# A decoder trunk in float32 on one Trainium2 core: seven products of sums in place of eight in the MLP's down-projection

## The chip, the core and the metric

The kernel runs on one core of one Trainium2 chip. The engines are TensorE (PE; PEld is its loading of weights), VectorE (DVE), ScalarE (ACT), GpSimd (POOL) and SyncE (SP, which issues nearly all DMAs here). The metric is the device time of one execution in microseconds (us), lower is better. A profile of one execution on the same chip gives the times of single instructions.

## The reference

Two layers. Each has a mixer (layer 0 an attention with forget gates, layer 1 a short gated convolution), a squared-ReLU MLP, and gated embeddings, with norms before and after each part. Sequence 512, width 1024, MLP width 4096, all in float32. The change concerns the MLP:

```python
def sq_relu_mlp(h, w_up, w_down):
    return jnp.square(jax.nn.relu(h @ w_up)) @ w_down

for i in range(2):
    ...                                   # mixer: x = x + rmsnorm(m, g[1])
    f = sq_relu_mlp(rmsnorm(x, g[2]), w_mlp_up[i], w_mlp_down[i])
    x = x + rmsnorm(f, g[3])
    ...                                   # gated embeddings
```

## The kernel before

**Products.** Each float32 operand is split into a high part `hi` (rounded to the matmul's fp32r form, a copy on ScalarE, L170) and a low part `lo` (source minus high part, a subtraction on VectorE, L171). `mm3` makes one product of three matmuls, `hi hi`, `lo hi` and `hi lo` (L162 to L164), all into one PSUM bank. There are eight banks of 128 x 512.

**The weight stream.** `plan` lists all weight tiles of 128 x 512 in the order of their use. `fetch` has SP load them into a ring of eight buffers (`raws`), `prepare` splits them into two pages (`wh`, `wl`), and `wide` and `narrow` hand a tile to a matmul, after they have prepared the next SOON = 8 tiles of the list. All other tiles of 128 x 512 come from a pool of PAGES = 76 pages. A tile scheduler sets the order of the instructions on each engine from the program and its own estimate of times; each engine then runs its list in order and waits on semaphores.

**The MLP.** `mlp` works through eight groups of 512 hidden columns. In a group, `up(gr)` makes four banks (index f, 128 hidden columns by all 512 tokens) of 8 x 3 matmuls each. From each bank come `r` = relu (ScalarE, L642), `hh` = its square rounded (ScalarE, L643), `q` = its square in full (VectorE, L645) and `hl` = q - hh (VectorE, L648). `down(gr, hs, t, n)` makes the bank of 128 tokens (t, four of them) by 512 output columns (n, two of them): four products over f, so 8 x 4 x 3 = 96 matmuls a group. A bank is added to the accumulator `acc[t, n]` on VectorE (L666; in group 0 copied there by ScalarE, L663). In group 0 the up stage runs in two halves of 256 tokens, since the norm before it ends block by block.

**Round about it.** `pre_norm` makes the normed input (`stats`, `rstd` with two small GpSimd instructions, L185 and L188, then `scaled` and a transposition that `put_off` defers and `need` calls in). `mixer_out` adds the mixer's output to the residual `xs` (eight pages, kept through the MLP like the gains g3 and g4). After group 7's bank pair of a token block come `squares`, `gained` and `residual`, and the next norm. `late` loads and splits the embeddings at group 7.

Of the kernel before, what the change touches and what calls it, by code (L numbers as in the profile page):

```python
# [49 lines left out]
def trunk(ctx: ExitStack, tc, x, pT, g, wv, wqk, bf, wo, wci, cw, wco, wup, wdn, wpp, wpg, out):  # L50
# [117 lines left out]
    def split(hi, lo, src):  # L168

        nc.scalar.copy(hi, src)  # L170
        nc.vector.tensor_tensor(out=lo, in0=src, in1=hi.bitcast(F32), op=ALU.subtract)  # L171
# [400 lines left out]
    def conv(hT):  # L572
# [49 lines left out]
        return lambda k, t: ys[k].at(lambda h: h[:, t * P : (t + 1) * P])  # L622

    def mlp(l, hT, xs, gB, then, late):
        acc = {}

        def up(gr):
            hs = {}
            for lo, hi in ((0, 256), (256, 512)) if gr == 0 else ((0, 512),):
                n = hi - lo  # L630
                for f in range(4):
                    need(*range(lo // P, hi // P))
                    ps = bank(f"up{l}_{gr}_{f}_{lo}")
# [8 lines left out]
                    nc.scalar.activation(r[:, :n], ps[:, :n], AF.Relu)  # L642
# [2 lines left out]
                    nc.vector.tensor_tensor(  # L645
                        out=sq[:, :n], in0=r[:, :n], in1=r[:, :n], op=ALU.mult
                    )
                    nc.vector.tensor_tensor(  # L648
# [188 lines left out]
```

## Time and profile before

| what | value |
|---|---|
| median of 3 executions | 1287.08 us (1285.12 to 1288.13) |
| the profiled execution's own time | 1285.32 us |
| its span, first to last instruction | 1283.6 us |
| mean granted clock of TensorE in it | 0.998 |
| PE busy | 1257.1 us in 6140 matmuls |
| VectorE, ScalarE, GpSimd busy | 709.7, 546.7, 151.2 us |
| moved by DMA | 140.24 MB |

In rows of the profile's groups, "out<-in" are names of the program with numbers left out, then sizes, the count after an x, and behind the bar the busy time in us, the mean of one in ns, and the idle time of the engine just before them with what ended it. A row of a timeline has its start in us, its duration in us, and then the same. A row of windows has, for each engine, the busy time and the number of instructions, then the granted clock and the share of the DMA engines.

### The profile page before, as it was taken

To read this page: it belongs to the slowest core of one execution; us is meant where nothing else is said; L and a number is where in the kernel's file an instruction comes from. 1 tells how busy PE (TensorE), PEld (TensorE's weight loads), DVE (VectorE), ACT (ScalarE), POOL (GpSimd) and SP (SyncE) were. 2 spreads that over 40 slices of the span, in tenths; PEclk is the share of its full clock that TensorE was granted. 3 is DMA by queue.
4 is the path that set the end of the run, shared out by engine and by line. 5 is a ranking of instruction groups with operands and counts; after the bars stand their busy time and mean duration, and the time that the engine had idled before them with its cause. 6 is when DMAs were issued, how large, how long until landed. Compare 5 with 4: busy or idle time off the path is not lost.

```text
span 1283.6 us, 17353 instructions
## 1 busy us (share of the span) xinstructions
PE 1257.1 (98%) x6140; PEld 1058.0 (82%) x6140; DVE 709.7 (55%) x1310; ACT 546.7 (43%) x1165; POOL 151.2 (12%) x267
## 2 busy tenths in 40 slices
PE   7999999999999999999999999999999999999997
PEld 6888888788888888888788988889888888888876
DVE  5557887573534553465867444455345444534773
ACT  5457776564422242234555233335423322432551
POOL 2026666120000000000211000010000000000120
PEclk9999999999999999999999999999999999999999
DMA  6455544533413431342323233423334123413401
GB/s 209 156 148 160 165 146 116 181 96 95 146 34 99 131 117 48 99 148 98 99 86 99 79 95 97 153 83 100 98 99 132 52 97 115 131 35 114 148 17 49
DMA packets 81174, 140.24 MB, mean 109 GB/s; under 512 B 9600, under 2 KB 16816, under 8 KB 81088
## 3 DMA queue, kind: packets, MB, share of 16 engines
q1 hardware_dynamic: 80880, 138.88, 34.8%
q8 instruction: 48, 0.79, 0.3%
q14 instruction: 38, 0.31, 0.1%
q10 hardware_dynamic: 144, 0.26, 0.1%
q0 software_dynamic: 64, 0.00, 0.0%
HBM read 132.73 MB, written 2.18 MB: 105 GB/s over the span
## 4 chain that ended last, share of the span: by engine, by line
PE 92%; DVE 3%; DMA 2%; ACT 1%; issue 1%; POOL 1%; SPq 0%; DVEq 0%; POOLq 0%; ACTq 0%
PE dn L163 9%; PE dn L162 9%; PE dn L164 9%; PE up L164 9%; PE up L162 9%; PE up L163 9%; PE qk L163 2%; PE qk L162 2%; PE qk L164 2%; PE pg L163 2%; PE pg L164 2%; PE pg L162 2%; PE pT L432 1%; PE c L164 1%; PE c L162 1%; PE u L164 1%
## 5 line engine op out<-in xcount | busy, mean ns | idle before, releaser
L171 DVE TENSOR_TENSOR wl<-raw,wh 128x512 fp32r<-128x512 f32 (+1 forms) x428 | 271.2, 686 | 49.6 <-ACT wh L170 48.8
L170 ACT CAST wh<-raw 128x512 fp32r<-128x512 f32 (+1 forms) x428 | 236.6, 614 | 23.7 <-DMA raw<-in_wdn 13.4
L163 PE MATMUL dn<-wh,hl 128*128 128x512 f32 x512 | 199.3, 389 | 0.0
L164 PE MATMUL dn<-wl,hh 128*128 128x512 f32 x512 | 199.3, 389 | 0.0
L642 ACT ACTIVATE r<-up 128x512 f32<-128x512 f32 (+1 forms) x72 | 39.7, 551 | 364.2 <-PE up L164 341.3
L162 PE MATMUL dn<-wh,hh 128*128 128x512 f32 x512 | 194.8, 389 | 0.0
L645 DVE TENSOR_TENSOR q<-r 128x512 f32<-128x512 f32 (+1 forms) x72 | 45.6, 633 | 210.0 <-ACT r L642 209.9
L666 DVE TENSOR_TENSOR acc<-dn,acc 128x512 f32<-128x512 f32 x112 | 76.9, 690 | 88.2 <-PE dn L164 88.2
L162 PEld LDWEIGHTS dn<-wh,hh 128*128 128x128 f32 x512 | 96.1, 188 | 20.0
L164 PEld LDWEIGHTS dn<-wl,hh 128*128 128x128 f32 x512 | 96.1, 188 | 19.9
L163 PEld LDWEIGHTS dn<-wh,hl 128*128 128x128 f32 x512 | 96.1, 188 | 19.8
L162 PE MATMUL up<-m0h,wh 128*128 128x512 f32 (+1 forms) x288 | 105.2, 366 | 1.4 <-ACT m0h L170 1.4
L162 PE MATMUL up<-m1h,wh 128*128 128x512 f32 (+1 forms) x288 | 105.1, 366 | 0.9 <-ACT m1h L170 0.9
L164 PE MATMUL up<-m0l,wh 128*128 128x512 f32 (+1 forms) x288 | 104.7, 366 | 0.9 <-DVE m0l L171 0.9
L163 PE MATMUL up<-m1h,wl 128*128 128x512 f32 (+1 forms) x288 | 105.0, 366 | 0.0
L163 PE MATMUL up<-m0h,wl 128*128 128x512 f32 (+1 forms) x288 | 105.0, 366 | 0.0
L164 PE MATMUL up<-m1l,wh 128*128 128x512 f32 (+1 forms) x288 | 104.5, 366 | 0.0
L185 POOL TENSOR_SCALAR mr_r_v<-fs,fs 128x1 f32<-128x1 f32 x8 | 3.9, 488 | 671.2 <-ACT junk L193 671.0
L162 PEld LDWEIGHTS up<-m0h,wh 128*128 128x128 f32 x288 | 54.3, 189 | 10.7 <-ACT m0h L170 1.9
L162 PEld LDWEIGHTS up<-m1h,wh 128*128 128x128 f32 x288 | 54.3, 189 | 9.9 <-ACT m1h L170 1.1
L164 PEld LDWEIGHTS up<-m0l,wh 128*128 128x128 f32 x288 | 54.1, 189 | 10.0 <-DVE m0l L171 1.3
L163 PEld LDWEIGHTS up<-m0h,wl 128*128 128x128 f32 x288 | 54.3, 189 | 8.7
(211 smaller groups left out, 2442.5 us busy)
## 6 DMA issues: line engine op xcount, KB each, us to landing
raw<-in_wup SPq DMA_DIRECT2D x128, 256.0 KB, 3.2
raw<-in_wdn SPq DMA_DIRECT2D x128, 256.0 KB, 4.0
raw<-in_wci SPq DMA_DIRECT2D x48, 256.0 KB, 3.2
raw<-in_wqk SPq DMA_DIRECT2D x32, 256.0 KB, 3.6
raw<-in_wpg SPq DMA_DIRECT2D x32, 256.0 KB, 3.4
g<-in_g SPq DMA_DIRECT2D x22, 256.0 KB, 5.2
prl<-neg_c SPq DMA_DIRECT2D x16, 256.0 KB, 6.0
raw<-in_wo SPq DMA_DIRECT2D x16, 256.0 KB, 3.2
```

Of the source, the lines that this page charges most:

```text
L162: nc.tensor.matmul(ps, a.hi, b.hi, start=start, stop=False)
L163: nc.tensor.matmul(ps, a.lo, b.hi, start=False, stop=False)
L164: nc.tensor.matmul(ps, a.hi, b.lo, start=False, stop=stop)
L170: nc.scalar.copy(hi, src)
L171: nc.vector.tensor_tensor(out=lo, in0=src, in1=hi.bitcast(F32), op=ALU.subtract)
L185: nc.gpsimd.tensor_scalar(out=v, in0=parts[0], scalar1=parts[1], scalar2=EPS, op0=ALU.add, op1=ALU.add)
L432: nc.tensor.transpose(ps[:, b * P : (b + 1) * P], probs[h][b][:, j * P : (j + 1) * P], ident)
L642: nc.scalar.activation(r[:, :n], ps[:, :n], AF.Relu)
L645: nc.vector.tensor_tensor(out=sq[:, :n], in0=r[:, :n], in1=r[:, :n], op=ALU.mult)
L666: nc.vector.tensor_tensor(out=a, in0=ps, in1=a, op=ALU.add)
```

## The change

In groups 0 to 6 of each layer the down-projection is a product of a 2 x 2 block matrix by another, made with seven products (Strassen's scheme in Winograd's form). A is the squared relu: A11 and A21 are the first and second half of the 512 tokens for an even f, A12 and A22 for the following odd f; the pair of f is counted by p (two in a group). B is the weight: rows r by the parity of f, columns by n. The sums are

```
S1 = A21 + A22   S2 = S1 - A11   S3 = A11 - A21   S4 = A12 - S2
T1 = B12 - B11   T3 = B22 - B12  T2 = B22 - T1    T4 = B21 - T2
products: 1: A11 B11   2: A12 B21   3: S4 B22   4: A22 T4   5: S1 T1   6: S2 T2   7: S3 T3
```

(T4 has the sign with which the combination needs additions only.) Each product has two banks (s, 128 tokens of the half each) and sums over p: 7 x 2 x 2 x 3 = 84 matmuls a group. The seven products are accumulated over groups 0 to 6 in 14 pages, and combined once per layer. Group 7 keeps the plain form, adds its banks to the combined totals, and has its first token block in another loop order. All sums T and S, the low parts of the T's and the combination run on GpSimd. The A side's high parts are copies on ScalarE of `q` and of the sums, with the low parts on VectorE. `raws` grows from 8 to 14 buffers, the pages go from 76 to 70. `xs` is written to DRAM after the mixer and read back before group 7, and g3 and g4 are loaded there.

```diff
-PAGES = 76
+PAGES = 70
+RAWS = 14
...
+PRODUCTS = {
+    1: ("A11", "B11"), 2: ("A12", "B21"), 3: ("S4", "B22"), 4: ("A22", "T4"),
+    5: ("S1", "T1"), 6: ("S2", "T2"), 7: ("S3", "T3"),
+}
+STEPS = (1, 2, 4, 5, 6, 7, 3)
...
+    def plan_down(l, gr):
+        at = {}
+        for name, r, c in (("B11", 0, 0), ("B21", 1, 0), ("B12", 0, 1), ("B22", 1, 1)):
+            for p in range(2):
+                at[name, p] = len(loads)
+                loads.append(wdn[l, c, 4 * gr + 2 * p + r])
+        for i in STEPS:
+            name = PRODUCTS[i][1]
+            for p in range(2):
+                where["dn", l, gr, name, p] = len(order)
+                order.append((("dn", l, gr, name, p), at if name[0] == "T" else at[name, p]))
+        derived[l, gr] = at
...
+    def derive(l, gr):
+        at = derived.pop((l, gr))
+        fetch(max(at.values()) + 1)
+        B = {key: fetched[n][:, :S] for key, n in at.items()}
+        for p in range(2):
+            for name, a, b in (("T1", "B12", "B11"), ("T3", "B22", "B12"), ("T2", "B22", "T1"),
+                               ("T4", "B21", "T2")):
+                t = page(f"{name}_{l}_{gr}_{p}")
+                derived[l, gr, name, p] = t
+                B[name, p] = t[:, :S]
+                nc.gpsimd.tensor_tensor(out=B[name, p], in0=B[a, p], in1=B[b, p], op=ALU.subtract)
...
-    def split(hi, lo, src):
+    def split(hi, lo, src, eng=nc.vector):
         nc.scalar.copy(hi, src)
-        nc.vector.tensor_tensor(out=lo, in0=src, in1=hi.bitcast(F32), op=ALU.subtract)
+        eng.tensor_tensor(out=lo, in0=src, in1=hi.bitcast(F32), op=ALU.subtract)
...
+        def quarters(gr, f, q, s, A):
+            L, R = slice(0, S // 2), slice(S // 2, S)
+            sums = lambda out, a, b, op: nc.gpsimd.tensor_tensor(out=out, in0=a, in1=b, op=op)
+            if f % 2 == 0:
+                halves(gr, f, ("A11",), q[f], A)
+                s[f] = page(f"s34{l}_{gr}_{f}")
+                sums(s[f][:, L], q[f][:, L], q[f][:, R], ALU.subtract)
+                return
+            left, right = q[f - 1], q[f]
+            halves(gr, f, ("A12", "A22"), right, A)
+            s12, s34 = page(f"s12{l}_{gr}_{f}"), s[f - 1]
+            sums(s12[:, L], left[:, R], right[:, R], ALU.add)
+            sums(s12[:, R], s12[:, L], left[:, L], ALU.subtract)
+            sums(s34[:, R], right[:, L], s12[:, R], ALU.subtract)
+            halves(gr, f, ("S1", "S2"), s12, A)
+            halves(gr, f, ("S3", "S4"), s34, A)
+
+        def down(gr, A):
+            for i in STEPS:
+                a_name, b_name = PRODUCTS[i]
+                banks = [bank(f"dn{l}_{gr}_{i}{s}") for s in range(2)]
+                for p in range(2):
+                    w = wide("dn", l, gr, b_name, p)
+                    for s in range(2):
+                        mm3(
+                            banks[s], A[a_name, p].at(lambda h: h[:, s * P : (s + 1) * P]), w,
+                            p == 0, p == 1,
+                        )
+                for s in range(2):
+                    if gr == 0:
+                        acc[i, s] = page(f"acc{l}_{i}_{s}")
+                        nc.scalar.copy(acc[i, s][:, :S], banks[s])
+                    else:
+                        a = acc[i, s][:, :S]
+                        nc.vector.tensor_tensor(out=a, in0=banks[s], in1=a, op=ALU.add)
+
+        def combine():
+            for s in range(2):
+                for to, i in ((2, 1), (6, 1), (7, 6), (4, 7), (6, 5), (3, 6), (5, 7)):
+                    a = acc[to, s][:, :S]
+                    nc.gpsimd.tensor_tensor(out=a, in0=a, in1=acc[i, s][:, :S], op=ALU.add)
...
+        gB = late()
+        total = combine()
...
+        for t in range(NB):
+            for n in range(2):
+                nc.sync.dma_start(kept[l, t, n], xs[t][n][:, :S])
+
+        def late():
+            for t in range(NB):
+                for n in range(2):
+                    xs[t][n] = page(f"xd{l}_{t}_{n}")
+                    nc.sync.dma_start(xs[t][n][:, :S], kept[l, t, n])
+            g3 = gain(l, 3)
+            g4.extend(gain(l, 4))
+            ps_in.extend(embeddings(l))
+            return g3
```

How it moves instructions shows in the engines' lists. Names carry the layer, the group and f or p, then a running number. GpSimd in layer 0, before: between the last statistics of the norm ahead of the MLP (`n20_r3`) and the first of the norm behind it (`mr0_r0`) its list has nothing.

```order
L185 TENSOR_SCALAR n20_r3_v_3674<-n20_q0_3_3670,n20_q1_3_3672 128x1
L188 TENSOR_TENSOR n20_r3_y_3675<-n20_r3_v_3674,neg_half_81 128x1
L185 TENSOR_SCALAR mr0_r0_v_6554<-fs0_0_0_6548,fs0_0_1_6550 128x1
L188 TENSOR_TENSOR mr0_r0_y_6555<-mr0_r0_v_6554,neg_half_81 128x1
L185 TENSOR_SCALAR n40_r0_v_6564<-n40_q0_0_6560,n40_q1_0_6562 128x1
L188 TENSOR_TENSOR n40_r0_y_6565<-n40_r0_v_6564,neg_half_81 128x1
```

GpSimd after, group 4 of layer 0, from the low parts of T4 and T1 on to those of T2 and T3:

```order
L217 TENSOR_TENSOR wl168_5611<-T4_0_4_0_5506,wh168_5610 128x512
L217 TENSOR_TENSOR wl169_5621<-T4_0_4_1_5514,wh169_5620 128x512
L217 TENSOR_TENSOR wl170_5631<-T1_0_4_0_5500,wh170_5630 128x512
L217 TENSOR_TENSOR wl171_5641<-T1_0_4_1_5508,wh171_5640 128x512
L705 TENSOR_TENSOR s340_4_2_5657<-q0_4_2_5481 128x256
L705 TENSOR_TENSOR s120_4_3_5691<-q0_4_2_5481,q0_4_3_5482 128x256
L705 TENSOR_TENSOR s120_4_3_5691<-s120_4_3_5691,q0_4_2_5481 128x256
L705 TENSOR_TENSOR s340_4_2_5657<-q0_4_3_5482,s120_4_3_5691 128x256
L217 TENSOR_TENSOR wl172_5706<-T2_0_4_0_5504,wh172_5705 128x512
L217 TENSOR_TENSOR wl173_5716<-T2_0_4_1_5512,wh173_5715 128x512
L217 TENSOR_TENSOR wl174_5730<-T3_0_4_0_5502,wh174_5729 128x512
L217 TENSOR_TENSOR wl175_5740<-T3_0_4_1_5510,wh175_5739 128x512
```

Where the list had gone straight from one norm to the next, it now has 24 instructions a group; here the sums of the second pair of f stand between the low parts of T4 and T1 and those of T2 and T3.

VectorE at the end of group 4's up stage and the beginning of its down stage, before:

```order
L645 TENSOR_TENSOR q0_4_2_0_5356<-r0_4_2_0_5353 128x512
L648 TENSOR_TENSOR hl0_4_2_5352<-q0_4_2_0_5356,hh0_4_2_5351 128x512
L645 TENSOR_TENSOR q0_4_3_0_5389<-r0_4_3_0_5386 128x512
L648 TENSOR_TENSOR hl0_4_3_5385<-q0_4_3_0_5389,hh0_4_3_5384 128x512
L171 TENSOR_TENSOR wl148_5396<-raw148_5393,wh148_5395 128x512
L171 TENSOR_TENSOR wl149_5405<-raw149_5402,wh149_5404 128x512
L171 TENSOR_TENSOR wl150_5414<-raw150_5411,wh150_5413 128x512
L171 TENSOR_TENSOR wl151_5423<-raw151_5420,wh151_5422 128x512
L171 TENSOR_TENSOR wl152_5476<-raw152_5473,wh152_5475 128x512
L171 TENSOR_TENSOR wl153_5485<-raw153_5482,wh153_5484 128x512
L171 TENSOR_TENSOR wl154_5494<-raw154_5491,wh154_5493 128x512
L666 TENSOR_TENSOR acc0_0_0_4061<-dn0_4_0_0_5392,acc0_0_0_4061 128x512
```

VectorE at the same place after:

```order
L677 TENSOR_TENSOR q0_4_2_5481<-r0_4_2_0_5650 128x512
L217 TENSOR_TENSOR A11l0_4_2_5654<-q0_4_2_5481,A11h0_4_2_5653 128x256
L677 TENSOR_TENSOR q0_4_3_5482<-r0_4_3_0_5684 128x512
L217 TENSOR_TENSOR A12l0_4_3_5688<-q0_4_3_5482,A12h0_4_3_5687 128x512
L217 TENSOR_TENSOR S1l0_4_3_5696<-s120_4_3_5691,S1h0_4_3_5695 128x512
L738 TENSOR_TENSOR acc0_1_0_4079<-dn0_4_10_5703,acc0_1_0_4079 128x512
L217 TENSOR_TENSOR S3l0_4_3_5700<-s340_4_2_5657,S3h0_4_3_5699 128x512
L738 TENSOR_TENSOR acc0_1_1_4081<-dn0_4_11_5704,acc0_1_1_4081 128x512
L738 TENSOR_TENSOR acc0_2_0_4105<-dn0_4_20_5727,acc0_2_0_4105 128x512
L738 TENSOR_TENSOR acc0_2_1_4107<-dn0_4_21_5728,acc0_2_1_4107 128x512
L738 TENSOR_TENSOR acc0_4_0_4131<-dn0_4_40_5751,acc0_4_0_4131 128x512
L217 TENSOR_TENSOR wl176_5754<-raw146_5496,wh176_5753 128x512
```

The low parts of the sums (`S1l`, `S3l`) stand between the squares and the accumulations, and the list waits there for GpSimd's sums `s12` and `s34`; the weights' low parts come behind the accumulations of products 1 and 2 (the first of them in the last row).

PE in group 4's down stage, before, where the last hidden block (`hh0_4_3`) is first used, 25 matmuls after the stage's first:

```order
L162 MATMUL dn0_4_2_0_5444<-wh141_5227,hh0_4_1_5294 128x512
L163 MATMUL dn0_4_2_0_5444<-wh141_5227,hl0_4_1_5295 128x512
L164 MATMUL dn0_4_2_0_5444<-wl141_5228,hh0_4_1_5294 128x512
L162 MATMUL dn0_4_2_0_5444<-wh142_5239,hh0_4_2_5351 128x512
L162 MATMUL dn0_4_0_0_5392<-wh143_5251,hh0_4_3_5384 128x512
L162 MATMUL dn0_4_1_0_5430<-wh143_5251,hh0_4_3_5384 128x512
L163 MATMUL dn0_4_2_0_5444<-wh142_5239,hl0_4_2_5352 128x512
```

PE at the corresponding place after, where the last hidden block (`A12h0_4_3`) is first used, 30 matmuls after the stage's first:

```order
L208 MATMUL dn0_4_11_5704<-wh165_5526,A11h0_4_2_5653 128x512
L210 MATMUL dn0_4_50_5775<-wl170_5631,S1h0_4_1_5601 128x512
L209 MATMUL dn0_4_10_5703<-wh165_5526,A11l0_4_2_5654 128x512
L210 MATMUL dn0_4_10_5703<-wl165_5527,A11h0_4_2_5653 128x512
L209 MATMUL dn0_4_11_5704<-wh165_5526,A11l0_4_2_5654 128x512
L210 MATMUL dn0_4_11_5704<-wl165_5527,A11h0_4_2_5653 128x512
L208 MATMUL dn0_4_51_5776<-wh170_5630,S1h0_4_1_5601 128x512
L209 MATMUL dn0_4_51_5776<-wh170_5630,S1l0_4_1_5602 128x512
L210 MATMUL dn0_4_51_5776<-wl170_5631,S1h0_4_1_5601 128x512
L208 MATMUL dn0_4_20_5727<-wh167_5546,A12h0_4_3_5687 128x512
L208 MATMUL dn0_4_21_5728<-wh167_5546,A12h0_4_3_5687 128x512
```

PE goes through the first pair of f for products 1, 2, 4 and 5 with eight banks open, and returns to them with the second pair; product 5's sum `S1` of the first pair and the low part `wl170` of T1 come before the last hidden block.

More of the change, by code (lines that the diff above doesn't have):

```diff
@@ L652, in up @@
-            return hs
-        def down(gr, hs, t, n):
-            ps = bank(f"dn{l}_{gr}_{t}_{n}")
-            for f in range(4):
-                mm3(
-                    ps, hs[f].at(lambda h: h[:, t * P : (t + 1) * P]),
-                    wide("dn", l, gr, n, f, soon=16 if gr == 7 else SOON), f == 0, f == 3,
-                )
-            if gr == 0:
-                acc[t, n] = page(f"acc{l}_{t}_{n}")
-                nc.scalar.copy(acc[t, n][:, :S], ps)
-            else:
-                a = acc[t, n][:, :S]
-                nc.vector.tensor_tensor(out=a, in0=ps, in1=a, op=ALU.add)
@@ L668, in mlp @@
-        for gr in range(8):
-            if gr == 7:
-                late()
-            hs = up(gr)
-            if gr < 7:
-                for n in range(2):
-                    for t in range(NB):
-                        down(gr, hs, t, n)
-            else:
-                for t in range(NB):
-                    for n in range(2):
-                        down(gr, hs, t, n)
-                    fs = [acc[t, n][:, :S] for n in range(2)]
-                    sums = [squares(f, f"fs{l}_{t}_{n}") for n, f in enumerate(fs)]
-                    mg = [gained(f, gB, n, None, acc[t, n]) for n, f in enumerate(fs)]
-                    residual(t, mg, sums, xs[t], f"mr{l}")
-                    then(t)
+                    done(f, lo, hi, r)
@@ new lines, in combine, with done @@
+        def combine():
[3 more added lines that the diff above has]
+                    nc.gpsimd.tensor_tensor(out=a, in0=a, in1=acc[i, s][:, :S], op=ALU.add)
+            return {
+                (2 * half + s, n): acc[i, s]
+                for s in range(2) for i, half, n in ((2, 0, 0), (3, 0, 1), (4, 1, 0), (5, 1, 1))
+            }
+        for gr in range(7):
+            A, s, q = {}, {}, {f: page(f"q{l}_{gr}_{f}") for f in range(4)}
+            def done(f, lo, hi, r):
+                square(q[f][:, lo:hi], r[:, : hi - lo])
+                if hi == S:
+                    quarters(gr, f, q, s, A)
+            up(gr, done)
+            down(gr, A)
@@ new lines, in mlp @@
+        for t in range(NB):
+            banks = [bank(f"dn{l}_7_{t}_{n}") for n in range(2)]
+            for f, n in [(f, n) for f in range(4) for n in range(2)] if t == 0 else [
+                (f, n) for n in range(2) for f in range(4)
+            ]:
+                w = wide("dn", l, 7, n, f, soon=12)
+                mm3(banks[n], tokens_of(hs[f], t), w, f == 0, f == 3)
+            for n in range(2):
+                a = total[t, n][:, :S]
+                nc.vector.tensor_tensor(out=a, in0=banks[n], in1=a, op=ALU.add)
+            fs = [total[t, n][:, :S] for n in range(2)]
+            sums = [squares(f, f"fs{l}_{t}_{n}") for n, f in enumerate(fs)]
+            mg = [gained(f, gB, n, None, total[t, n]) for n, f in enumerate(fs)]
+            residual(t, mg, sums, xs[t], f"mr{l}")
+            then(t)
```

96 lines of the change are left out of this document (57 added, 39 removed).

## The prediction

> **What bounds the kernel now.** The page comes first, with its engine totals, the slices and the chain that ended last.
>
> ```profile
> span 1283.6 us, 17353 instructions
> ...
> PE 1257.1 (98%) x6140; PEld 1058.0 (82%) x6140; DVE 709.7 (55%) x1310; ACT 546.7 (43%) x1165; POOL 151.2 (12%) x267
> ...
> POOL 2026666120000000000211000010000000000120
> ...
> PE 92%; DVE 3%; DMA 2%; ACT 1%; issue 1%; POOL 1%; SPq 0%; DVEq 0%; POOLq 0%; ACTq 0%
> ```
>
> PE is busy for 98% of the span and carries 92% of the chain. GpSimd stands nearly idle through the MLPs (the zeros in its slices), and that is where the new work goes. Next I cut one steady group of the MLP by window: its up stage, its down stage, and as a third window one whole period of a group (a down stage with the up stage behind it).
>
> ```profile
> core 0: us, PE busy (x) PEld busy (x) DVE busy (x) ACT busy (x) POOL busy (x), PEclk, DMA share, GB/s
> 359.35:381.10 21.75, 21.75 (x97) 18.02 (x96) 7.25 (x11) 5.77 (x10) 0.00 (x0) 1.00 0.15 48
> 381.10:402.86 21.76, 21.76 (x97) 18.02 (x96) 13.17 (x21) 7.88 (x14) 0.00 (x0) 1.00 0.45 146
> ...
> 337.58:381.10 43.52, 43.52 (x193) 36.05 (x192) 20.43 (x32) 13.64 (x24) 0.00 (x0) 1.00 0.30 97
> ```
>
> PE fills the whole window at the full granted clock (1.00): 192 matmuls in 43.52 us, 0.2267 us apiece. DVE works 20.4 us of it, ACT 13.6, GpSimd none. So a matmul less is 0.2267 us less, as long as the other engines deliver in time.
>
> **What it removes.** Seven products take 7 x 2 x 2 x 3 = 84 matmuls of 512 columns where the plain down stage takes 96. Over groups 0 to 6 of two layers: 14 x 12 = 168 fewer, 168 x 0.2267 = 38.1 us. A group becomes 21.76 + 84 x 0.2267 = 40.8 us. That is the new beat that every other engine must keep.
>
> **What it adds on DVE and ACT.** Prices come from the groups by form in the same period of 43.5 us, and one 256-wide row from the whole run.
>
> ```profile
> L171 DVE TENSOR_TENSOR wl<-raw,wh 128x512 fp32r<-128x512 f32 x16 | 10.0, 686 | 0.0
> L666 DVE TENSOR_TENSOR acc<-dn,acc 128x512 f32<-128x512 f32 x8 | 5.5, 690 | 7.9 <-PE dn L164 7.9
> ...
> L645 DVE TENSOR_TENSOR q<-r 128x512 f32<-128x512 f32 x4 | 2.8, 693 | 14.8 <-ACT r L642 14.8
> ...
> L170 ACT CAST wh<-raw 128x512 fp32r<-128x512 f32 x16 | 8.9, 616 | 1.3 <-DMA raw<-in_wdn 1.0
> ...
> L642 ACT ACTIVATE r<-up 128x512 f32<-128x512 f32 x4 | 2.4, 598 | 28.5 <-PE up L164 28.5
> ```
>
> ```profile
> L648 DVE TENSOR_TENSOR hl<-q,hh 128x256 fp32r<-128x256 f32 x16 | 6.8, 425 | 1.9 <-DVE q L645 0.5
> ```
>
> DVE per group: 14 low parts of weights (8 up tiles, B11, B21, B22 twice each), 4 squares, 6 low parts of 512 columns for A12/A22, S1/S2, S3/S4, 2 of 256 for A11: 24 x 0.69 + 2 x 0.425 = 17.4 us; 14 accumulations instead of 8: 14 x 0.69 = 9.7. Sum 27.1 of 40.8. ACT: 22 weight casts, 4 relus, 6 copies of 512, 2 of 256 below 0.62 each: 32 x 0.62 + 4 x 0.60 less the half of two, about 21. Both have room, so they cost nothing, unless an instruction is late for its matmul.
>
> **What it adds on GpSimd.** Per group 16 subtractions of 512 columns (8 for T1 to T4, 8 for their low parts) and 8 sums of 256. The trace has no such operation on GpSimd; the nearest rows:
>
> ```profile
> L425 POOL TENSOR_SCALAR prl<-prl,rs 128x512 f32<-128x512 f32 x16 | 26.7, 1667 | 12.6 <-DVE rs L424 12.6
> ...
> L425 POOL TENSOR_SCALAR pr<-pr,rs 128x256 f32<-128x256 f32 x16 | 16.2, 1014 | 0.8 <-DVE rs L424 0.7
> ...
> L535 POOL TENSOR_SCALAR_AFFINE_SELECT ones<-ones 128x512 f32<-128x512 f32 x1 | 0.6, 612 | 0.1
> ```
>
> The low end is 0.61 us at 512 (one input, no arithmetic). The others are arithmetic with one wide input, 1.67 in the mean; undisturbed ones take 1.57, and three meetings with DVE show why:
>
> ```profile
> 114.25 1.57 POOL L425 TENSOR_SCALAR prl<-prl,rs 128x512 f32<-128x512 f32 x1 [0.35 <-DVE rs L424]
> 114.50 0.98 DVE L171 TENSOR_TENSOR wl<-raw,wh 128x512 fp32r<-128x512 f32 x1
> ...
> 151.30 0.69 DVE L171 TENSOR_TENSOR wl<-raw,wh 128x512 fp32r<-128x512 f32 x1
> 151.55 1.89 POOL L425 TENSOR_SCALAR prl<-prl,rs 128x512 f32<-128x512 f32 x1
> ...
> 169.61 1.56 POOL L425 TENSOR_SCALAR prl<-prl,rs 128x512 f32<-128x512 f32 x1
> 169.71 1.12 DVE L171 TENSOR_TENSOR wl<-raw,wh 128x512 fp32r<-128x512 f32 x1
> ```
>
> At 256 columns an undisturbed one, and one beside a pair of DVE's subtractions:
>
> ```profile
> 148.88 0.92 POOL L425 TENSOR_SCALAR pr<-pr,rs 128x256 f32<-128x256 f32 x1
> ...
> 165.87 1.28 DVE L171 TENSOR_TENSOR wl<-raw,wh 128x512 fp32r<-128x512 f32 x2
> ...
> 166.01 1.85 POOL L425 TENSOR_SCALAR pr<-pr,rs 128x256 f32<-128x256 f32 x1
> ```
>
> When GpSimd came first, DVE's 0.69 became 0.98 and 1.12: DVE got going only 114.50 + 0.29 - 114.25 = 0.54 us after GpSimd's start, and 0.53 in the other case. When DVE came first, GpSimd's 1.57 became 1.89, so DVE shut it out for 0.25 + 0.32 = 0.57 us. The two hold something in common, GpSimd for 0.54 of its 1.57 us, DVE for 0.57 of its 0.69. A second wide input then adds at most another 0.54: high end 1.57 + 0.54 = 2.11 at 512, and 0.92 + 0.27 = 1.19 at 256. I take 1.57 and 0.92, the row of the same engine, width and kind. GpSimd per group: 16 x 1.57 + 8 x 0.92 = 32.5 us of 40.8 (low end 16 x 0.61 + 8 x 0.31 = 12.3; high end 16 x 2.11 + 8 x 1.19 = 43.3). Time of the common thing: GpSimd 16 x 1.08 + 8 x 0.54 = 21.6 with two inputs, DVE 24 x 0.57 + 2 x 0.3 = 14.3; 35.9 of 40.8. It fits, with meetings that stretch single instructions by some 0.3 us.
>
> The Trainium skill's page "GPSIMD Engine Reference", section 3.1, measures a two-input add at 4497 ns for 2048 columns; an estimate from that is 1.12 us at 512, inside my ends, and the sum stays as it is. No run so far shows it.
>
> **Does each operand come in time?** The hand-over from up to down:
>
> ```profile
> 380.87 0.39 PE L164 MATMUL up<-m0l,wh 128*128 128x512 f32 x1
> ...
> 381.10 0.39 PE L162 MATMUL dn<-wh,hh 128*128 128x512 f32 x1
> ...
> 381.30 0.60 ACT L642 ACTIVATE r<-up 128x512 f32<-128x512 f32 x1 [4.18 <-PE up L164]
> ...
> 381.93 0.69 DVE L645 TENSOR_TENSOR q<-r 128x512 f32<-128x512 f32 x1 [3.95 <-ACT r L642]
> ...
> 382.73 0.69 DVE L648 TENSOR_TENSOR hl<-q,hh 128x512 fp32r<-128x512 f32 x1
> ```
>
> Counted from the start of an up stage, the last square is ready 0.83 + 0.69 us after down begins, at 23.3. The order puts A12's f = 3 half at the 31st matmul, 6.8 us into the stage; its chain takes 1.5 + 0.62 + 0.69 = 2.8. S1 of f = 3 is used 42 matmuls in, 9.5 us; its chain is 1.5, two GpSimd sums 1.84, copy and low part 1.3: 4.7. GpSimd's queue in order: four sums from 23.3 to 27.0, then low parts of T2, T2, T3, T3 at 28.6, 30.1, 31.7, 33.3, used 52, 59, 65 and 71 matmuls in: 33.5, 35.1, 36.5, 37.9. Then eight T sums, to 45.9, which is 5.1 us into the next group; four sums when the second square is there (12.4) to 16.1; low parts of T4, T4, T1, T1 by 22.4, first used at 24.9. So every operand in a steady group has 2.8 us or more, and most have 4.5. In front of the waiting sums in GpSimd's queue lies nothing that a matmul needs earlier. PE waits for nothing: cost 0, covered by those microseconds.
>
> Fourteen accumulations free their banks before the next up stage needs them, for all 14 lie within the 13.7 us of free DVE time. Products 1, 2, 4 and 5 hold all eight banks for 48 matmuls; product 6 can begin with the first one drained, 0.69 us.
>
> **Where the cover is thin.** The first group of each layer has GpSimd's T sums behind the last statistics of the norm:
>
> ```profile
> 275.53 0.30 POOL L185 TENSOR_SCALAR n_r_v<-n_q,n_q 128x1 f32<-128x1 f32 x1 [3.17 <-ACT junk L193]
> 275.91 0.56 POOL L188 TENSOR_TENSOR n_r_y<-n_r_v,neg_half 128x1 f32<-128x1 f32 x1
> ```
>
> ```profile
> 294.03 0.40 PE L162 MATMUL dn<-wh,hh 128*128 128x512 f32 x1
> ```
>
> From 276.5 eight T sums last to 289.0; the four sums wait for a square at about 290.4, to 294.1; T4's low part is ready at 295.7 (used 14 matmuls in, 297.2), T1's at 298.8 (22 in, 299.0). That is no slack, and each meeting with DVE costs 0.3: between 0 and 2 us, I take 1.0 per layer. In group 1 the order puts two accumulations ahead of A12's last low part on DVE: 0 to 1.5, I take 0.7. Over two layers 2 x 1.7 = 3.4.
>
> **x in DRAM.** Eight writes after the mixer and eight reads plus gains at group 7, of 256 KB like these:
>
> ```profile
> raw<-in_wup SPq DMA_DIRECT2D x128, 256.0 KB, 3.2
> raw<-in_wdn SPq DMA_DIRECT2D x128, 256.0 KB, 4.0
> ```
>
> On SP's queue the last writes wait for the last residual, with loads of group 1's weights behind them, which are wanted 20 us later. The reads have a whole up stage (21.8 us) before the first residual. DMA is busy for 0.30 of a period; eight more beside sixteen make 0.45 in one group. Cost 0 behind that stage, one landing time (3 to 4 us) if it failed. The 14 combining sums per layer, 14 x 1.57 = 22, lie on GpSimd during group 7's up stage of 21.8 us, with 24 matmuls and their hand-over more before the first is added to.
>
> **Sum.** 1285.3 is the profiled execution (its span and 1.7 around it); less 38.1, plus 3.4: 1250.6. The median shown (1287.08) lies 1.8 above that execution: 1252.4.
>
> **Rivals.** (1) GpSimd loses time at each meeting: 24 instructions times 0.3 is 7.2, so 39.7 of 40.8, and the instruction at 166.01, beside a pair, lost 0.93. The idle stretches before the squares (8 us) can't all be used, so PE would wait between half a microsecond and 2 in each group: 7 to 28 on top of the forecast, 1259 to 1280. Against it: 4.5 us of slack, and that all the meetings would have to fall before the last low parts.
>
> (2) A second input costs its full 0.54: GpSimd becomes the bound at 43.3 against the 43.5 of before: 1287.1 - 14 x 0.2 + 3.4 = 1288, no change. It needs more than 1.97 us at 512 to matter at all (1.57 x 40.8 / 32.5).
>
> (3) The other side: the common thing is held for the whole instruction once a second input is read, so GpSimd and DVE take turns: 32.5 + 17.4 = 49.9 per group, 1287.1 + 14 x 6.4 = 1377. In general 16a + 8 x 0.586a + 17.4 for a price of a; slower than before from a = 1.26 on (43.5). The three meetings speak against it, for DVE ran while GpSimd's 1.57 us went on; they had one wide input, though. This is the Trainium skill's rule in "SBUF — State Buffer", "Who interferes with whom": a DVE instruction with two inputs in SBUF contends with one of GpSimd that reads SBUF, and whoever starts first has the shared port pair for its whole instruction. This case's rows agree on who contends and not on how long (0.54 of 1.57 us); by that rule the time would be that of this rival.
>
> **Chances and range.** My forecast 0.57, its own range 1247 (a little under no stalls at all, 1249) to 1259; rival (1) 0.24; rival (2), within 0.2% or 2.6 us, about what a measurement of this kernel can tell, 0.04; rival (3), with what ends between 1290 and its 1377, 0.15. So faster 0.81, same 0.04, slower 0.15. The range takes the first two cases and a little beyond: 1246 to 1284.
>
> **What would show it.** A group lasting 40.8 us with PE full in the windows; GpSimd's 512-wide subtraction between 1.1 and 1.7 us and its busy time 25 to 34 per group; DVE's two-input instructions at 0.7 to 0.9 in the mean; waits of PE for S or T low parts only in groups 0 and 1. Wrong if a group's period is above 42, with PE waiting for GpSimd's low parts in every one, or DVE's low parts at 1.5 us or more.

## The result, and the profile after

The changed kernel takes 1257.4 us (1255.4 to 1258.8 in 4 runs) against 1286.9: a ratio of 0.9771, 95% interval 0.9753 to 0.9788. The profiled execution of it has a span of 1255.4 us, 28.2 less than before. The page after, in the lines that answer to those of before:

```profile
span 1255.4 us, 17998 instructions
...
PE 1225.2 (98%) x5972; PEld 1026.9 (82%) x5972; DVE 907.3 (72%) x1402; ACT 611.5 (49%) x1309; POOL 627.0 (50%) x631
...
POOL 2027677147868677774311000016777777878120
...
PE 80%; DVE 8%; DMA 4%; ACT 3%; issue 3%; POOL 2%; SPq 0%; DVEq 0%; POOLq 0%; ACTq 0%
```

PE is still the engine that fills the span. GpSimd went from 151 to 627 us, VectorE from 710 to 907. Three steady groups of layer 0, cut by window, one period each:

```profile
core 0: us, PE busy (x) PEld busy (x) DVE busy (x) ACT busy (x) POOL busy (x), PEclk, DMA share, GB/s
439.17:479.97 40.80, 40.80 (x182) 33.79 (x180) 33.79 (x43) 18.10 (x34) 32.19 (x25) 1.00 0.37 108
479.97:520.77 40.80, 40.80 (x181) 33.79 (x180) 33.92 (x40) 18.20 (x34) 33.28 (x26) 1.00 0.35 112
520.77:561.57 40.80, 40.80 (x182) 33.79 (x180) 32.75 (x42) 16.11 (x30) 31.16 (x25) 1.00 0.33 100
```

A period is 40.80 us with PE full, as 180 matmuls need. GpSimd's groups and two of VectorE's in the same three periods:

```profile
L217 POOL TENSOR_TENSOR wl<-T,wh 128x512 fp32r<-128x512 f32 x24 | 35.7, 1518 | 7.5 <-ACT wh L216 7.5
L127 POOL TENSOR_TENSOR T<-raw,T 128x512 f32<-128x512 f32 x12 | 19.6, 1631 | 0.5
...
L217 DVE TENSOR_TENSOR wl<-raw,wh 128x512 fp32r<-128x512 f32 x43 | 45.6, 1109 | 0.0
L738 DVE TENSOR_TENSOR acc<-dn,acc 128x512 f32<-128x512 f32 x44 | 28.1, 678 | 2.2 <-PE dn L210 2.2
```

VectorE's weight subtraction has gone from 0.69 to 1.11 us in the mean, while the accumulation, which has only one input in SBUF, stays at 0.68. Single instructions from the timeline: one of GpSimd's alone, then a stretch where the two engines alternate, then two of GpSimd's alone:

```profile
456.11 0.74 POOL L705 TENSOR_TENSOR s<-q,s 128x256 f32<-128x256 f32 x1
...
441.86 1.62 POOL L127 TENSOR_TENSOR T<-raw,T 128x512 f32<-128x512 f32 x1
442.26 1.77 DVE L217 TENSOR_TENSOR wl<-raw,wh 128x512 fp32r<-128x512 f32 x1
443.44 1.74 POOL L127 TENSOR_TENSOR T<-raw,raw 128x512 f32<-128x512 f32 x1
443.95 1.78 DVE L217 TENSOR_TENSOR wl<-raw,wh 128x512 fp32r<-128x512 f32 x1
...
567.27 2.53 POOL L745 TENSOR_TENSOR acc<-acc,acc 128x512 f32<-128x512 f32 x2
```

Alone, GpSimd takes 0.74 us at 256 columns, and two of 512 run through in 2.53, so 1.27 to 1.30 each. Where both are busy they take turns: VectorE's starts are 1.69 us apart, with one of GpSimd's in between, and each lasts 1.6 to 1.8. With VectorE's share of 0.57 (the prediction's), an estimate is that GpSimd holds what they share for 1.69 - 0.57 = 1.12 us of its 1.30.

**Where the 38.1 us went.** The first matmul of each stage in the two traces, less what the missing matmuls should save:

| stage | before | after | later than 12 matmuls less would be |
|---|---|---|---|
| up to the first MLP | 266.8 | 267.1 | 0.3 |
| layer 0, group 0 | 49.0 | 48.9 | 2.6 |
| layer 0, group 1 | 43.5 | 41.6 | 0.8 |
| layers 0 and 1, groups 2 to 6 | 43.5 each | 40.8 each | 0 |
| layer 0, embeddings, convolution | 198.0 | 200.9 | 2.9 |
| layer 1, the mixer's output | 45.3 | 45.3 | 0 |
| layer 1, groups 0 and 1 | 91.3 | 87.1 | 1.3 |
| group 7, layer 0 and layer 1 | 43.5, 43.5 | 43.6, 44.5 | 1.0 |
| layer 1, embeddings and the end | 67.4 | 68.5 | 1.1 |

The last column, before rounding, sums to 9.9, and 38.1 - 9.9 = 28.2, the difference of the spans. Part of it is what PE waited for: its idle time (span less busy time) grew from 26.5 to 30.2 us. The first two rows are from before, the others from after:

```profile
PE pg L163 <- DVE p1l L171: 0.9, 1, 0.9
PE pg L163 <- DVE p0l L171: 0.9, 1, 0.9
```

```profile
PE pg L209 <- DVE p1l L217: 1.9, 1, 1.9
PE pg L209 <- DVE p0l L217: 1.9, 1, 1.9
PE dn L209 <- DVE A11l L217: 1.7, 1, 1.7
PE c L210 <- DVE cl L217: 1.4, 1, 1.4
...
PE dn L209 <- DVE hl L771: 0.6, 1, 0.6
```

No row names GpSimd in the MLP: what is late is VectorE's work, in group 0 (A11l) and at the layers' ends (hl, p0l, p1l, cl).

The rest lies in PE's busy time, which is 1225.2 us and not 1257.1 - 38.1 = 1219.0. A matmul is shown 0.39 us long while the next one starts 0.23 us after it, so the first 0.16 us of a wait look busy. And in the embeddings of layer 0 PE's clock was cut. The stretch from the first matmul `pg` on, before and after, then PE's rows after:

```profile
626.83:648.00 21.17, 20.28 (x101) 16.60 (x100) 16.58 (x27) 13.57 (x30) 4.14 (x7) 1.00 0.16 51
611.46:632.00 20.54, 18.63 (x87) 15.15 (x86) 15.91 (x25) 10.85 (x26) 4.74 (x9) 0.92 0.13 39
```

```profile
617.57 0.39 PE L210 MATMUL pg<-wl,p0h 128*128 128x512 f32 x1
617.80 0.40 PE L208 MATMUL pg<-wh,p0h 128*128 128x512 f32 x1
620.10 0.70 PE L209 MATMUL pg<-wh,p0l 128*128 128x512 f32 x1 [1.91 <-DVE p0l L217]
...
622.31 0.63 PE L209 MATMUL pg<-wh,p0l 128*128 128x512 f32 x1
622.74 0.63 PE L210 MATMUL pg<-wl,p0h 128*128 128x512 f32 x1
```

Behind the wait for p0l the matmuls start 0.43 us apart instead of 0.23, and the granted clock of the stretch is 0.92 instead of 1.00. The embeddings of layer 0 take 64.1 us instead of 61.6: 1.0 of these 2.5 us is longer waiting, and about 1.5 is this slower stretch. In layer 1 a wait of the same length (p1l, 1.9) was not followed by one, so what sets it off stays open.

### The profile page after: what moved, and what is told of

The parts are those of the page before. It is cut to its first block, busy times and chain, and to the rows that moved or that the text cites. A ratio compares the mean times of both kernels' runs of the same rounds, so it can differ in the third digit from the quotient of the medians.

```text
span 1255.4 us, 17998 instructions
## 1 busy us (share of the span) xinstructions
PE 1225.2 (98%) x5972; PEld 1026.9 (82%) x5972; DVE 907.3 (72%) x1402; ACT 611.5 (49%) x1309; POOL 627.0 (50%) x631
## 4 chain that ended last, share of the span: by engine, by line
PE 80%; DVE 8%; DMA 4%; ACT 3%; issue 3%; POOL 2%; SPq 0%; DVEq 0%; POOLq 0%; ACTq 0%
PE up L210 8%; PE up L208 8%; PE up L209 8%; PE dn L209 7%; PE dn L210 7%; PE dn L208 7%; DVE wl L217 2%; PE qk L209 2%; PE qk L208 2%; PE qk L210 2%; ACT junk L239 2%; PE pg L209 1%; PE pg L210 1%; PE pg L208 1%; PE c L210 1%
## 5 line engine op out<-in xcount | busy, mean ns | idle before, releaser
L217 DVE TENSOR_TENSOR wl<-raw,wh 128x512 fp32r<-128x512 f32 (+1 forms) x400 | 355.0, 937 | 26.9 <-ACT wh L216 26.1
L216 ACT CAST wh<-raw 128x512 fp32r<-128x512 f32 (+1 forms) x400 | 217.9, 620 | 7.4 <-DVE xd L289 7.2
L217 POOL TENSOR_TENSOR wl<-T,wh 128x512 fp32r<-128x512 f32 x112 | 163.0, 1486 | 33.0 <-ACT wh L216 31.7
L738 DVE TENSOR_TENSOR acc<-dn,acc 128x512 f32<-128x512 f32 x168 | 106.9, 678 | 6.5 <-PE dn L210 6.5
L127 POOL TENSOR_TENSOR T<-raw,raw 128x512 f32<-128x512 f32 x56 | 87.2, 1569 | 36.0 <-DMA raw<-in_wdn 19.6
L127 POOL TENSOR_TENSOR T<-raw,T 128x512 f32<-128x512 f32 x56 | 91.1, 1627 | 2.2
L677 DVE TENSOR_TENSOR q<-r 128x512 f32<-128x512 f32 (+1 forms) x72 | 70.6, 989 | 23.8 <-ACT r L691 23.8
L216 ACT CAST wh<-T 128x512 fp32r<-128x512 f32 x112 | 61.4, 618 | 3.9 <-POOL T L127 3.9
L210 PEld LDWEIGHTS up<-m1l,wh 128*128 128x128 f32 x288 | 54.1, 189 | 9.1 <-DVE m1l L217 0.3
L209 PEld LDWEIGHTS up<-m1h,wl 128*128 128x128 f32 x288 | 54.4, 189 | 8.8
```

The costliest lines, as they stand in the source:

```text
L127: nc.gpsimd.tensor_tensor(out=B[name, p], in0=B[a, p], in1=B[b, p], op=ALU.subtract)
L209: nc.tensor.matmul(ps, a.lo, b.hi, start=False, stop=False)
L210: nc.tensor.matmul(ps, a.hi, b.lo, start=False, stop=stop)
L217: eng.tensor_tensor(out=lo, in0=src, in1=hi.bitcast(F32), op=ALU.subtract)
L677: nc.vector.tensor_tensor(out=out, in0=r, in1=r, op=ALU.mult)
L738: nc.vector.tensor_tensor(out=a, in0=banks[s], in1=a, op=ALU.add)
```

## The experiments

**The memory side alone.** The kernel before, with x kept in DRAM, the gains loaded late, 14 raw buffers and 70 pages:

```diff
-PAGES = 76
+PAGES = 70
-    raws = pool("raws", 8)
+    raws = pool("raws", 14)
...
+                nc.sync.dma_start(kept[l, t, n], xs[t][n][:, :S])
...
+                    nc.sync.dma_start(xs[t][n][:, :S], kept[l, t, n])
```

> The kernel before with the memory side of the change alone: x written to DRAM after the mixer and read back at group 7, g3 and g4 loaded there, 14 raw buffers, 70 pages; the down stages are plain, 96 matmuls. Theory A (transfers are hidden): as before, 1287 us within 2.6, and the stage of the gated embeddings lasts 61.6 and 67.4 us as before. Rival B (the late reads of x and of the gains are what delays the layers' ends in the changed kernel, by 2.5 and 1.1 us in that stage and about 1 us in group 7): 1290 to 1292 us, with that stage at 64 us in layer 0.

1286.5 us, ratio 0.9996 (0.9987 to 1.0005): Theory A. By itself this side of the change costs nothing; the embeddings' stages last 61.3 and 67.1 us.

**Without the combining sums.**

```diff
-            for s in range(2):
-                for to, i in ((2, 1), (6, 1), (7, 6), (4, 7), (6, 5), (3, 6), (5, 7)):
-                    a = acc[to, s][:, :S]
-                    nc.gpsimd.tensor_tensor(out=a, in0=a, in1=acc[i, s][:, :S], op=ALU.add)
```

> The changed kernel without the 28 combining sums of 512 columns on GpSimd (left out, so group 7 adds its banks to the raw sums of products 2 to 5); every other instruction stands in the same order. Theory A (these sums meet VectorE's instructions during group 7's up stage, VectorE arrives 4 to 5 us late at the first token block, and the end of the layer pays): 1252 to 1254 us, the low part of the squared relu of f = 3 within 2.5 us of the down stage's start instead of 5.9, the embeddings' stages near 61.6 and 67.4 us. Rival B (the end of the layer is late for another reason, as the loads of x): 1257 us within 2.

1252.4 us, 5.0 less: Theory A in the time (embeddings' stages 61.1 and 67.1 us). But the low part of f = 3 was still 4.4 us behind the down stage's start, not 2.5, so something else was late as well. PE's clock is not cut in layer 0's embeddings here (1.00 from 611 to 631 us), so about 1.5 of the 5.8 us between the two profiled spans (1255.4 and 1249.6) are that. ScalarE's timeline in group 7 of the changed kernel (up stage from 561.57) shows it:

```profile
573.09 0.62 ACT L216 CAST pth<-pt 128x512 fp32r<-128x512 f32 x1 [17.75 <-DMA pt<-in_pT]
577.03 0.62 ACT L216 CAST pth<-pt 128x512 fp32r<-128x512 f32 x1 [3.33 <-DMA pt<-in_pT]
577.56 2.18 ACT L216 CAST wh<-raw 128x512 fp32r<-128x512 f32 x4
579.64 0.59 ACT L691 ACTIVATE r<-up 128x512 f32<-128x512 f32 x1
```

The first relu of the stage runs at 579.6, though its bank is full at 567.0. It stands in ScalarE's list behind the split of the embeddings, and these were loaded on SP behind eight reads of x and four gains.

**The embeddings loaded first.**

```diff
         def late():
+            ps_in.extend(embeddings(l))
             for t in range(NB):
...
-            ps_in.extend(embeddings(l))
```

> The changed kernel with the loads of the embeddings (pt) issued on SP ahead of the eight reads of x and the four gains at group 7. In the changed kernel ScalarE's list has the split of pt ahead of group 7's relus and stood for 17.8 us, until pt had landed behind those reads, so every relu and square of that stage came about 12 us late. Theory A (that stall takes up the slack, and the combining sums on GpSimd then make the layer's end late): with the stall gone the end of the layer recovers what leaving out the sums gave: 1252 to 1254 us, embeddings' stages near 61.5 and 67.3 us. Rival B (the sums' meetings alone are the cause): 1256 to 1258 us. Rival C (x lands too late for the first residual): above 1258.

1253.4 us (1252.7 to 1255.2), 4.0 less: Theory A. ScalarE's first wait is down from 17.75 to 7.08:

```profile
563.14 0.62 ACT L216 CAST pth<-pt 128x512 fp32r<-128x512 f32 x1 [7.08 <-DMA pt<-in_pT]
...
570.69 0.59 ACT L691 ACTIVATE r<-up 128x512 f32<-128x512 f32 x1
```

The embeddings' stages take 60.9 and 66.2 us, 0.7 and 1.2 less than before the change. Not all is cured: in group 7 PE still waits 1.1 and 0.7 us for the low part of the squared relu, and layer 0's down stage takes 23.4 us there instead of 21.8. Most of the loss at the layers' ends needed both: the late relus alone cost nothing (the memory side by itself has a like wait, 14.7 us), and the sums alone cost little.

**The combining sums on VectorE.**

```diff
-                    nc.gpsimd.tensor_tensor(out=a, in0=a, in1=acc[i, s][:, :S], op=ALU.add)
+                    nc.vector.tensor_tensor(out=a, in0=a, in1=acc[i, s][:, :S], op=ALU.add)
```

> The changed kernel with the 28 combining sums (14 a layer) on VectorE instead of GpSimd. Leaving them out altogether gave 1252.4 us against 1257.4. Theory A (on GpSimd they cost VectorE about 1.1 us a meeting during group 7's up stage; on VectorE they cost 0.69 each, with no meeting): VectorE saves 14 x 0.4 = 6 us a layer there, about half of the loss comes back: 1254 to 1256 us. Rival B (VectorE's list gets 9.7 us longer in a stage where it is behind already, so the layers' ends come as late or later): 1257 to 1262 us.

1253.4 us (1252.6 to 1254.1): a little better than Theory A, against B. 9.7 more microseconds of VectorE's own work per layer cost less than the sums on GpSimd had. That was not by fourteen meetings: in layer 0's group 7 the changed kernel's sums stretched four of VectorE's instructions, by 0.7 to 1.1 us, and VectorE stood idle for 6.1 us before the split of the embeddings, with room for them there.

**The T subtractions twice.**

```diff
+                for _ in range(2):
                     nc.gpsimd.tensor_tensor(out=B[name, p], in0=B[a, p], in1=B[b, p], op=ALU.subtract)
```

> The changed kernel with each of the eight T subtractions of a group issued twice on GpSimd, into the same page: 8 more instructions of 512 columns with two wide inputs. Theory A (GpSimd and VectorE share one thing, which GpSimd's 512-wide subtraction holds for about 1.13 of its 1.30 us and VectorE's for 0.57 of 0.69): held for 24 x 1.13 + 8 x 0.57 + 14.3 = 46.0 us a group instead of 37, PE waits in each group, 14 x 5.2 = 73 us more: 1310 to 1335 us. Rival B (each engine's own time counts, meetings only stretch single instructions): GpSimd's own 24 x 1.30 + 8 x 0.74 = 37.1 us still lies under 40.8: 1257 to 1262 us.

1404.4 us, ratio 1.0915 (1.0893 to 1.0938). Rival B falls at once; Theory A had the direction and half the size. Two steady periods:

```profile
478.18:528.93 50.75, 44.78 (x181) 35.92 (x180) 38.56 (x42) 18.09 (x34) 43.45 (x32) 0.90 0.28 87
528.93:579.52 50.59, 44.91 (x181) 35.99 (x179) 37.93 (x42) 18.08 (x34) 43.30 (x33) 0.90 0.28 92
```

GpSimd is busy for 43.4 of 50.7 us; the other 7 are waits inside its own list, which stands in an order that nothing can overtake. The sum of shared time (46.0) counted none of them. PE's granted clock is at 0.90 in these windows, and PE is busy for 44.8 us with the work of 40.8; how much of the period that adds stays open.

**Memsets instead.**

```diff
+                for _ in range(2):
+                    nc.gpsimd.memset(B[name, p], 0.0)
                 nc.gpsimd.tensor_tensor(out=B[name, p], in0=B[a, p], in1=B[b, p], op=ALU.subtract)
```

> The changed kernel with two memsets of 512 columns on GpSimd ahead of each of the eight T subtractions of a group, into the same page: 16 instructions of about 0.53 us, 8.4 us a group, that write and read nothing. GpSimd's own time comes to 26.7 + 8.4 = 35.1 us. Theory A (what is shared is the reading): VectorE's weight subtractions keep their mean of 1.1 us in the steady groups, and the time stays within 1257 to 1262 us. Rival B (any instruction of GpSimd holds it): 37 + 8.4 = 45.4 us a group, 1257 + 14 x 4.6 = 1320 us.

1299.4 us, ratio 1.011 (1.0076 to 1.0144): neither number. Three steady periods took 42.7 us each; one of them, then two groups and the waits of GpSimd over all three:

```profile
448.73:491.48 42.75, 41.68 (x182) 33.56 (x180) 33.73 (x41) 18.11 (x34) 38.11 (x41) 1.00 0.32 100
```

```profile
L128 POOL MEMSET T<- 128x512 f32 x49 | 23.2, 525 | 0.0
...
L219 DVE TENSOR_TENSOR wl<-raw,wh 128x512 fp32r<-128x512 f32 x43 | 43.1, 1049 | 0.0
```

```profile
POOL s L707 <- DVE q L679: 5.7, 3, 1.9
POOL wl L219 <- PE dn L210: 3.8, 3, 1.3
POOL wl L219 <- ACT wh L218: 3.8, 3, 1.3
```

The memsets themselves meet nobody: 0.525 us as alone (0.526 before), and VectorE's weight subtraction is at 1.05, not above the 1.11 of the changed kernel. From 300 to 560 us, 42 of VectorE's instructions of 512 columns with two inputs in SBUF ran beside memsets alone, and none took more than 0.69 us. That part of Theory A holds: an instruction of GpSimd that only writes does not take part. What binds is GpSimd's list: 38.1 us busy and 13.3 / 3 = 4.4 of waits make 42.5 a period. If the same waits are put to the changed kernel, an estimate is 33 + 4.4 = 37.4 of 40.8, so some 3.4 us to spare per group. The 1.9 us a period make 27 of the 42 us; group 7 takes 52.0 and 52.4 us instead of 43.6 and 44.5, and why stays open.

**Low parts of the T's on VectorE.**

```diff
-                raw, eng, w = derived.pop(key[1:]), nc.gpsimd, S
+                raw, eng, w = derived.pop(key[1:]), nc.vector, S
```

> The changed kernel with the low parts of T1 to T4 on VectorE, 8 a group taken from GpSimd. GpSimd's busy time falls from 33 to some 20 us a group. The shared time is 8 x 1.13 + 8 x 0.57 + 32 x 0.57 + 0.6 = 32.5 us a group instead of 37, VectorE's own time 27.1 + 5.5 = 32.6. Theory A (what matters is the shared time, and 37 of 40.8 was near its edge): the steady groups keep 40.8 us with fewer stretched instructions, group 0 and 1 wait less, 1254 to 1257 us. Rival B (VectorE is the tighter engine, and its list delays A's low parts and the accumulations): PE waits in each group, 1260 to 1275 us.

1251.8 us (1250.3 to 1253.2), ratio 0.9732: 5.6 less than the changed kernel, more than Theory A said. GpSimd is busy for 22 us a period, VectorE for 35 with eight instructions more, instead of 34. Group 0's down stage lost 2.1 of its 2.6 us of lateness, and the embeddings' stages are at 61.9 and 67.7.

**Group 0 without T subtractions**, memsets in their place:

```diff
+                if gr == 0:
+                    if name in ("T1", "T4"):
+                        nc.gpsimd.memset(B[name, p], 0.0)
+                    else:
+                        nc.gpsimd.memset(B[name, p], 1.0)
+                    continue
```

> The changed kernel with the eight T subtractions of group 0 in each layer replaced by eight memsets of the T pages (left out: the values of T in group 0). Theory A (in group 0 these subtractions meet VectorE's norm, squares and low parts, so A11's and A12's low parts come late: 2.6 us in layer 0, 0.5 in layer 1): VectorE's squares of 256 columns take 0.42 us again instead of 1.5 and group 0 loses its wait: 1254 to 1255.5 us. Rival B (group 0 waits because GpSimd's list starts late, behind the norm's statistics, with the low parts of T): no more than 1 us less, 1256 to 1258 us.

1257.7 us, but from 1254.0 to 1260.2 in five runs, and the spread goes with the granted clock: 1254.0 and 1254.1 us at 0.997 and 0.996, 1257.7 and 1258.1 at 0.993, 1260.2 at 0.992. The changed kernel's runs had 0.995 to 0.997; the two runs with such a clock lie where Theory A put them, the median does not. The trace says more: group 0's down stage takes 19.07 us in both layers instead of 22.29 and 19.69, and the squares on which the low parts of A11 and A12 wait are down to 0.42 us. First the changed kernel's group 0, five squares in a row (four of about 1.5 us) beside GpSimd's low parts of T, then the squares of this run:

```profile
288.96 6.03 POOL L217 TENSOR_TENSOR wl<-T,wh 128x512 fp32r<-128x512 f32 x4
...
289.48 6.14 DVE L677 TENSOR_TENSOR q<-r 128x256 f32<-128x256 f32 x5
```

```profile
284.07 2.62 DVE L683 TENSOR_TENSOR q<-r 128x256 f32<-128x256 f32 x2
288.28 0.42 DVE L683 TENSOR_TENSOR q<-r 128x256 f32<-128x256 f32 x1 [1.58 <-ACT r L697]
289.48 0.44 DVE L683 TENSOR_TENSOR q<-r 128x256 f32<-128x256 f32 x1 [0.44 <-ACT r L697]
```

So meetings are the cause of group 0's wait, as Theory A says, but for the squares it has the partner wrong. They met the low parts of T, which the T subtractions had pushed back to 289 us. Here the low parts begin at 280.5, and the two squares that still meet them take 2.62 us together; with the low parts on VectorE (the run above), group 0's squares took 0.41 each. Group 1's down stage then took 0.9 and 1.0 us longer than in the changed kernel, which gave part back.

**Half of them earlier** (the last argument is p).

```diff
             if (t, n) == (2, 0):
                 prepare(where[kind, 1, KT - 1] + 1 + SOON)
+                derive(0 if kind == "o" else 1, 0, 0)
```

> The changed kernel with half of group 0's T subtractions (p = 0, four per layer) placed ahead of the last two token blocks' norm statistics in GpSimd's list, where GpSimd idled for 6.0 us. Theory A (fewer meetings with VectorE in group 0's up stage): 1254 to 1256.5 us. Rival B (the four subtractions, 5.2 us, delay the statistics of the third token block, and PE waits for its turned block): 1258 to 1262 us.

1262.6 us (1259.4 to 1262.8): just above Rival B. Group 0's up stages grew from 26.6 to 30.6 and from 25.9 to 28.6 us, while its down stages had their 19.07. The idle stretch of GpSimd lay beside the norm of the last two blocks, where VectorE could not wait. The next statistics on GpSimd came at 274.2 instead of 269.7, but had stood 3.0 us for ScalarE's sums of VectorE's residual: the delay went through VectorE's list, not through GpSimd's as Rival B says. In layer 0 PE waits 1.7 us more in that up stage, and its granted clock there is 0.94 instead of 1.00.

**Combinations.** Low parts and combining sums on VectorE:

> The changed kernel with the low parts of T1 to T4 and the combining sums on VectorE; GpSimd keeps the T subtractions and the sums of the A side. Alone, these gave 1251.8 and 1253.4 us against 1257.4. Theory A (the low parts cured groups 0 and 1 and, by fewer meetings before group 7, most of the layer's end; the sums cured the layer's end alone): the gains overlap, 1249 to 1251.5 us. Rival B (VectorE's list is too long where group 6 ends and group 7 begins): 1252 to 1256 us.

1250.8 us (1249.6 to 1252.1), Theory A. With the embeddings loaded first as well:

> All three edits together: low parts of T and combining sums on VectorE, pt loaded ahead of x. The forecast without any stall in groups 0 and 1 was 1249. Theory A: 1248 to 1250.5 us. Rival B (pt was hidden once the other two were made): the same as with those two within 1.5 us.

1249.0 us (1248.7 to 1249.6), ratio 0.971 (0.9696 to 0.9723), Theory A: 8.4 us below the changed kernel, and what 1287.1 less 38.1 makes. It beats both kernels. All that was left on GpSimd per group, the T subtractions, on VectorE too:

```diff
-                nc.gpsimd.tensor_tensor(out=B[name, p], in0=B[a, p], in1=B[b, p], op=ALU.subtract)
+                nc.vector.tensor_tensor(out=B[name, p], in0=B[a, p], in1=B[b, p], op=ALU.subtract)
```

> As the version with low parts of T and combining sums on VectorE and pt loaded first (1249.0 us), with the eight T subtractions of a group on VectorE too; GpSimd keeps the eight sums of 256 columns. VectorE's own time is 40 x 0.69 + 2 x 0.425 + 14 x 0.68 = 38.0 us of 40.8 a group, without the meetings with GpSimd's 512-wide subtractions. Theory A (without meetings VectorE's own time counts, and 38.0 fits): 1249 to 1254 us, VectorE's weight subtractions near 0.70 us. Rival B (2.8 us of room is less than the waits inside VectorE's list, so PE waits in every group): 1260 to 1290 us.

1260.1 us (1258.2 to 1261.7), at the lower edge of Rival B, with half of Theory A true:

```profile
L217 DVE TENSOR_TENSOR wl<-raw,wh 128x512 fp32r<-128x512 f32 x42 | 26.5, 683 | 0.0
```

Without GpSimd's wide subtractions VectorE's are at 0.68 us again, and the steady groups take 40.8 to 41.2 us, so PE loses 0.4 in most of them. The largest loss is in one place, group 0's up stage in layer 0, 31.8 us instead of 26.6:

```profile
266.47:298.26 31.79, 28.56 (x208) 27.74 (x209) 23.76 (x42) 14.82 (x35) 6.77 (x10) 0.89 0.26 85
```

PE waits 2.4 us more there than in the changed kernel, and its granted clock is 0.89 instead of 1.00, which makes some 3.4 of the 31.8 us. Seven of the T subtractions run there, from 277.6 to 282, ahead of the low part of the third normed block; which of the waits that follow is due to them stays open. GpSimd is of use, with about two thirds of what the change gave it (22 of 32 us a period).

## Why the prediction was right, and where it was off

The forecast was 1252.4, within 1247 to 1259 for its likeliest case; the time was 1257.4.

- **168 matmuls, 38.1 us, 40.8 a group.** Right to the hundredth in the steady groups, 40.80 with PE full. The 1249.0 of the version with all three edits agrees too, partly by luck: group 0's down stage in layer 0 still takes 20.2 us instead of 19.0, and the embeddings' stages are 0.6 us shorter each than before the change.
- **GpSimd's price.** Total right (32.5 forecast, 31.2 to 33.3 measured), parts wrong, and that is luck: 1.27 to 1.30 alone, not 1.57 (and not the 1.12 that the prediction estimated beside its sum), plus 5 to 6 us of meetings that the forecast had put on top. The sum of the shared time, 35.9, was sound: 2 x 0.54 for two inputs against some 1.12. That would fit a hold that goes by what is read; no run changed the number of inputs alone.
- **VectorE.** Forecast 27.1, measured 33 to 34: the meetings cost it 6.7 us in 24 instructions, about the 0.3 each that was named, but uneven: 1.08 when it comes second, nothing when it comes first. Over the rows of 512 columns with two inputs in SBUF the mean in the steady groups is 1.01 us, so the sign that the prediction named (0.7 to 0.9) was missed.
- **Slack in steady groups.** Right that PE waits for nothing. The forecast gave the operands 2.8 us or more, most of them 4.5; the room of GpSimd's list was about 3.4 us, the estimate from the memsets.
- **Groups 0 and 1.** 3.4 forecast, 4.7 measured (2.6, 0.8, 0.5, 0.8). The place was right, the releaser wrong, so that the size came near is luck: the forecast had PE wait for T's low parts, and what came late was A11's on VectorE, after squares which those low parts on GpSimd had stretched from 0.42 to 1.5 us.
- **x in DRAM and the combining sums, cost 0.** These terms failed, together. The first asked when x lands, and x was in time. It did not ask what else stands behind twelve transfers on SP: the embeddings, whose split stands ahead of the relus in ScalarE's list. With the combining sums, to which the forecast gave room because GpSimd had it, the layers' ends lost 5.0 us (2.9, 1.0, 1.1), of which about 1.5 is PE's cut clock, a cost that the sum had no term for. These 5.0, 1.3 in groups 0 and 1, and 0.3 ahead of the first MLP make up, but for rounding, the 6.5 us by which the span (1255.4) is longer than the forecast's (1283.6 - 38.1 + 3.4 = 1248.9).
- **Rival 3, what is shared held for the whole instruction.** The price came out at 1.30, above the 1.26 from which this rival decides, and the time still went the other way: alternating instructions need 1.69 us a pair, not 1.30 + 0.69 = 1.99. The margin is smaller than that looks: two of VectorE's alone run through in 1.29 us (before, at 383.34) and two of GpSimd's in 2.53, so their own starts lie 0.60 and 1.23 us apart, 1.83 together. The rule of "SBUF — State Buffer", section "SBUF: two separate sides" of the Trainium skill (the first to start has the pair of ports for its whole instruction) is much nearer here, some 1.12 of 1.30 us, than in the rows of before, 0.54 of 1.57. There it does not hold: in the first meeting VectorE's subtraction ended at 115.48, ahead of GpSimd's instruction, which had begun first and ended at 115.82.
- **Rival 1, PE waits in each group.** It didn't, but it was near: 8.4 us more of GpSimd's work a group brought it, 42.7 us a period.

## What to carry to other kernels

An idle engine is not free when its instructions and a busy engine's take turns, as here: price each two-input instruction of GpSimd twice, for itself (1.30 us) and for the neighbour it stops (about 1.1), and place them where the neighbour has room, not where GpSimd has. Of an engine that works through its list in order, the waits inside the list count as well as its work; the bound comes when both together fill the beat. And when transfers are added to a queue, look at what stands behind them and at the list of the engine that receives it: here twelve loads put ahead of the embeddings held up ScalarE's relus for 12 us, though the change touched neither the embeddings nor the relus.
